# The input projection's 36 column chunks: a 512- and a 256-column product per weight tile in place of three of 256 columns, with the two bank halves added on evacuation

## The chip, the cores and the metric

The kernel runs on one core of a Trainium2 chip. The time is device microseconds of that core for one launch; the times below are of three runs, and one further execution was taken with the hardware profiler. TensorE (PE in the rows, its weight loads PEld) multiplies, VectorE (DVE) and ScalarE (ACT) do the elementwise work, SyncE (SP) issues the DMAs, GpSimd (POOL) does almost nothing.

## The reference, cut to what matters

One layer of a hybrid trunk, 256 tokens of width 2048, in float32:

```python
h = _rmsnorm(x, norm_mix[i])
proj = h @ w_in[i]
(s_x, s_z, s_b, s_c, s_dt, g_q, g_k, g_v, g_g, g_gk) = jnp.split(proj, split_pts, axis=-1)
y_ssd = _ssd_mixer(s_x, s_z, s_b, s_c, s_dt, ...)   # causal conv, silu, chunked scan, gate, norm
y_gla = _gla_mixer(g_q, g_k, g_v, g_g, g_gk, ...)   # gated linear attention, 4 heads, norm, gate
x = x + jnp.concatenate([y_ssd, y_gla], axis=-1) @ w_out[i]
h = _rmsnorm(x, norm_ffn[i])
u = _causal_dwconv(h @ ffn_w_up[i], ffn_conv_w[i], ffn_conv_b[i])
gate, val = jnp.split(u, [D_FF], axis=-1)
x = x + (jax.nn.silu(gate) * val) @ ffn_w_down[i]
pg = jax.nn.sigmoid(_rmsnorm(x, norm_ple[i]) @ ple_w_gate[i])
x = x + pg * (p[i] @ ple_w_proj[i])
return _rmsnorm(x, norm_final)
```

## The kernel before, in words

Every projection multiplies float32 numbers as sums of two rounded parts, a high and a low one: hi x hi + hi x lo + lo x hi. Weights arrive in chunks of 1 MB ([128, 2048], sixteen tiles of 128x128 side by side; the "v" chunks are [128, 1408]). `load` fetches a chunk into one of four `raw` buffers and `prepare` splits it in two halves, each with a cast on ACT (L185, `whi`) and a subtraction on DVE (L186, `wlo`); there are five buffers each of `whi` and `wlo`, so five halves. Activations lie as [128, 2, 256] tiles: the high parts of the 256 tokens, and behind them the low parts.

The input projection walks through the list `PLAN`: 12 value chunks "v" (in which the weights are the moving operand, L893 to L895, 352 columns, 24 products in a chunk) and 36 others: conv8 to conv11, conv0, v4, conv1, v5, conv2, v6, conv3, v7, conv4, q0, k0, conv5, v8, conv6, v9, conv7, v10, q1, k1, v11, q2, k2, q3, k3, z0 to z7, g0 to g7. Each of these 36 makes 128 output columns for all tokens, in 16 steps (k0 to k15, one weight tile each) of `mm3`: three products of 256 columns into the first half of a PSUM bank. `mm2`, used in the output, up, down and gate projections that follow, does the same with a 512-column product (hi x both parts, into both halves of the bank) and a 256-column one (lo x hi, into the first half); there `combine` adds the halves, with a copy on ACT (L229) and an add on DVE (L230). When a chunk is done its evacuation runs: `ev_conv` (scale by the norm, causal convolution, L526 to L531, then `half_silu`: tanh L436 on ACT, L437 on DVE), `ev_qk` (L727), `ev_z` (L699), `ev_g` (L838).

Between the steps stand "helper" matmuls of the two mixers and the norms. TensorE's order is fixed by the program: every fourth step calls `tick`, which resumes at most one of the tasks that are due; a task issues its next piece and yields a number of ticks. `mark` makes a result available to waiting tasks some ticks later. So the helper's place in TensorE's row is counted in steps, and TensorE waits there if the operand is late. ACT and DVE are ordered by a scheduler, in which weights (`load`) and norms have priority, and each takes its instructions strictly in that order.

The helpers that the prediction speaks of: the norms (`norm_task`, `gla_token` and `gla_norm`): L285 sums squares over partitions, DVE finds the inverse root with small operations (L288 to L298, then its high and low part L303 and L305), ACT makes two diagonal matrices per part (L310), and two matmuls L318 spread the result over the partitions; behind the norms of the GLA heads DVE scales the head (L807) and `ev_g` multiplies the gate in (L843, then `split`, L265). The decays of the scan (`decay_src`: eight ACT operations L582; `decay`: matmuls L589 and L590, then the exponential L592 on ACT); `decay` number i is followed by the sources of number i + 2. And L600, four transposes of convolved tiles (`ssd_xdt`).

Of the kernel before, what the change touches and what calls it, by code (L numbers as in the profile page):

```python
# [12 lines left out]
ALU = mybir.AluOpType  # L13
PSUM = bass.MemoryType.PSUM

T = 256
KT = 16
# [80 lines left out]
def trunk(ctx, tc, wst, wv, xin, pin, prm_d, cst_d, gku_d, out):  # L98
    nc = tc.nc
    V, S, G, PE = nc.vector, nc.scalar, nc.gpsimd, nc.tensor  # L100
# [15 lines left out]
    def tmp():  # L116
        return small.tile([128, T], F32, name="tmp", bufs=10)
# [31 lines left out]
    def mark(key, lag=5):  # L149
        done[key] = now[0] + lag  # L150
# [59 lines left out]
    def lhs(wt, j):  # L210
        hi, lo = wt[j // 8]
        w = slice((j % 8) * 128, (j % 8 + 1) * 128)
        return hi[:, w], lo[:, w]

    def mm2(ps, wt, j, act, first, last):
        hi, lo = lhs(wt, j)
        both = act.rearrange("p a t -> p (a t)")
        PE.matmul(ps, lhsT=hi, rhs=both, start=first, stop=False)  # L218
        PE.matmul(ps[:, 0:T], lhsT=lo, rhs=act[:, 0, :], start=False, stop=last)  # L219

    def mm3(ps, wt, j, act, first, last):
        hi, lo = lhs(wt, j)
        PE.matmul(ps, lhsT=hi, rhs=act[:, 0, :], start=first, stop=False)  # L223
        PE.matmul(ps, lhsT=hi, rhs=act[:, 1, :], start=False, stop=False)  # L224
        PE.matmul(ps, lhsT=lo, rhs=act[:, 0, :], start=False, stop=last)  # L225

    def combine(ps):
        t = tmp()
        S.copy(out=t, in_=ps[:, T:2 * T])  # L229
        V.tensor_tensor(out=t, in0=ps[:, 0:T], in1=t, op=ALU.add)  # L230
        return t
# [20 lines left out]
    def pcol(i):  # L252
        return prm[:, i:i + 1]
# [114 lines left out]
    for m in range(KT):  # L368
        wt = ready[m // 8]
        if m % 2 == 0:  # L370
            ps = pmt() if m % 4 == 0 else pxt()
# [4 lines left out]
    xa = []  # L376
# [28 lines left out]
    state = {}  # L405
# [116 lines left out]
    cT = slot()  # L522

    def ev_conv(i, ps):
        v = tmp()
        V.tensor_tensor(out=v, in0=ps[:, 0:T], in1=state["rh"], op=ALU.mult)  # L526
        c = tmp()
        S.activation(out=c, in_=v, func=AF.Identity, scale=pcol(P_CW + 36 + i),
                     bias=cbh[:, i:i + 1])
        for s in (1, 2, 3):  # L530
            V.scalar_tensor_tensor(out=c[:, s:], in0=v[:, :T - s],  # L531
                                   scalar=pcol(P_CW + 12 * (3 - s) + i), in1=c[:, s:],
                                   op0=ALU.mult, op1=ALU.add)
        if i < 8:
            if i % 2 == 0:
                state["xs"] = slot()
            ssd_x[i] = state["xs"][:, (i % 2) * T:(i % 2 + 1) * T]
            half_silu(c, ssd_x[i])
        elif i < 10:
            half_silu(c, bT[:, (i - 8) * T:(i - 7) * T])  # L540
        else:
            half_silu(c, cT[:, (i - 10) * T:(i - 9) * T])
        mark(("conv", i), 12)
# [109 lines left out]
    def ssd_front():  # L653
        yield from gates()
        yield from wait(*[("conv", 8 + i) for i in range(4)])
        ssd_bc()
        yield 1
        ssd_bt()
        for g in range(2):
            order = [(hg, c) for hg in (2 * g, 2 * g + 1) for c in range(2)]  # L660
            if g == 1:
                yield from wait(("y", 0))
            decay_src(*order[0])
            decay_src(*order[1])
            yield 3
            for i, o in enumerate(order):
                yield 4
                decay(*o)
                if i < 2:
                    decay_src(*order[i + 2])  # L670
            mark(("mt", g))
# [23 lines left out]

    def ev_z(i, ps):
        assert ("y", i // 4) in done
        zz = tmp()
        V.tensor_tensor(out=zz, in0=ps[:, 0:T], in1=state["rh"], op=ALU.mult)  # L699
        sz = tmp()  # L700
        half_silu(zz, sz)
        V.tensor_tensor(out=ssd_y[i], in0=ssd_y[i], in1=sz, op=ALU.mult)
        if i % 4 == 0:
            ssd_sq[i // 4] = SumSq()
        ssd_sq[i // 4].add(ssd_y[i])
        mark(("z", i), 7)

    def ssd_norm():
        for g in range(2):
# [14 lines left out]

    def ev_qk(dst, i, ps, sc):
        t = dst[i // 2][:, (i % 2) * T:(i % 2 + 1) * T]
        V.scalar_tensor_tensor(out=t, in0=ps[:, 0:T], scalar=sc, in1=state["rb"],  # L727
                               op0=ALU.mult, op1=ALU.mult)

    def gla_scale(h):  # L730
# [103 lines left out]
                yield 2  # L834

    def ev_g(i, ps):
        gg = tmp()
        V.tensor_tensor(out=gg, in0=ps[:, 0:T], in1=state["rh"], op=ALU.mult)  # L838
        sg = tmp()
        half_silu(gg, sg)  # L840
        assert ("o", i // 2) in done
        o = gla["o", i // 2][:, (i % 2) * T:(i % 2 + 1) * T]
        V.tensor_tensor(out=o, in0=o, in1=sg, op=ALU.mult)  # L843
        mix[8 + i] = split(o)
# [16 lines left out]
    for ci, (kind, i) in enumerate(PLAN):  # L861
        if ci == 0:
            late_loads()
        if ci > 2:
            wt = chunk(N_PROJ + ci)
        else:
            wt = ready.pop(N_PROJ + ci)
        if ci == 3:
            late_work()
        if ci >= 6:  # L870
            for o, t in stores[0:2]:
                dma(o, t)
            del stores[0:2]
            ordered[0] = bool(stores)
        if ci == 4:
            start(norm_task(sq_mix, 2048, in_norm, 7))
            start(ssd_front())
            start(ssd_rest())
            start(gla_front())
            start(gla_back())  # L880
            start(ssd_norm())
        if kind == "v":
            nb, kc = divmod(i, 4)
            if kc == 0:
                vps = [pmt(), pmt()]
            for kk in range(4):
                k = kc * 4 + kk
                hi, lo = wt[kk // 2]
                w = slice((kk % 2) * VB, (kk % 2 + 1) * VB)
                for c in range(2):  # L890
                    tk = slice(c * 128, (c + 1) * 128)
                    o = vps[c][:, 0:VB]
                    PE.matmul(o, lhsT=xa[k][:, 0, tk], rhs=hi[:, w], start=k == 0, stop=False)  # L893
                    PE.matmul(o, lhsT=xa[k][:, 0, tk], rhs=lo[:, w], start=False, stop=False)  # L894
                    PE.matmul(o, lhsT=xa[k][:, 1, tk], rhs=hi[:, w], start=False, stop=k == KT - 1)  # L895
                tick()
            if kc == 3:
                pend.append(lambda a=(nb, vps): ev_v(*a))
                flush()
        else:  # L900
            ps = pmt()
            for k in range(KT):
                mm3(ps[:, 0:T], wt, k, xa[k], k == 0, k == KT - 1)
                if k % TICK == TICK - 1:
                    tick()
            pend.append(lambda a=(kind, i, ps): ev_in(*a))
            flush()
# [156 lines left out]
    with tc.high_priority(offset=PRIO):  # L1064
        v, t = [small.tile([128, 2], F32, name=n, bufs=2) for n in ("rv", "rt")]
# [105 lines left out]
```

## Time and profile before

| what | value |
|---|---|
| time, median of 3 runs | 1241.51 us (1240.69 to 1241.93) |
| the profiled execution's own time | 1241.76 us |
| its span | 1240.0 us |
| mean granted clock of TensorE | 0.998 of full |
| busy: PE, PEld, DVE, ACT | 1228.7, 1103.7, 896.3, 692.1 us |
| chain that ended last | 96% PE |

Busy time is the union of an engine's instructions; matmuls overlap, so their durations add up to more, and what counts is the distance from one start to the next. The input projection's matmuls lie between 18 and 314 us of the span, the output projection from 314 to 404, the up and down projections to 1147, the gate to the end.

### The profile page before, as it was taken

The page shows a single profiled execution, that of the slowest core. Times are in us where ns is not written, and L with a number is a line of the kernel's source. Part 1 is how long each engine was busy: PE and PEld are TensorE (multiplying, and loading weights), DVE is VectorE, ACT ScalarE, POOL GpSimd, SP SyncE. Part 2 cuts the span into 40 slices and gives each one's busy share as a digit, 9 for nine tenths or more (in the row PEclk, how much of TensorE's full clock was granted, in tenths as well). Part 3 has the DMA queues.
Part 4 walks back from the last instruction along what each step waited for, and adds up shares of the span by engine and source line. Part 5 has one row for each costly group of instructions (what it writes and reads, how often), then busy time and mean ns, then how long its engine had stood idle before and what let it go on. Part 6 is the DMA issues. An engine that isn't in the chain of part 4 may idle for free.

```text
span 1240.0 us, 19470 instructions
## 1 busy us (share of the span) xinstructions
PE 1228.7 (99%) x7707; PEld 1103.7 (89%) x7707; DVE 896.3 (72%) x1531; ACT 692.1 (56%) x1144; POOL 3.0 (0%) x10
## 2 busy tenths in 40 slices
PE   9999999999999999999999999999999999999997
PEld 7999999999888888888888888888888888888886
DVE  7877565778677788887786555788777886666775
ACT  8685564566455565555553333555555554444664
POOL 0000000000000000000000000000000000000000
PEclk9999999999999999999999999999999999999999
DMA  8745353445555555555555555555555555556531
GB/s 328 297 144 194 129 203 108 160 147 176 194 176 198 174 200 182 192 197 180 201 179 195 191 183 203 176 198 188 186 200 177 201 183 208 196 179 228 198 134 68
DMA packets 36829, 231.00 MB, mean 186 GB/s; under 512 B 4209, under 2 KB 4593, under 8 KB 11138
## 3 DMA queue, kind: packets, MB, share of 16 engines
q1 hardware_dynamic: 36738, 229.76, 52.3%
q8 instruction: 60, 0.98, 0.3%
q14 instruction: 31, 0.25, 0.1%
HBM read 225.55 MB, written 4.19 MB: 185 GB/s over the span
## 4 chain that ended last, share of the span: by engine, by line
PE 96%; ACT 1%; DVE 1%; DMA 1%; SPq 0%; issue 0%; DVEq 0%
PE pm_t L218 49%; PE pm_t L219 24%; PE pm_t L223 6%; PE pm_t L225 6%; PE pm_t L224 6%; PE pm_t L894 1%; PE pm_t L895 1%; PE pm_t L893 1%; DMA raw<-in_wst_dram 1%; PE px_t L626 1%; ACT xg L257 0%; ACT whi L185 0%; PE px_t L789 0%; ACT tmp L278 0%; PE px_t L285 0%; SPq L165 0%
## 5 line engine op out<-in xcount | busy, mean ns | idle before, releaser
L185 ACT CAST whi<-raw 128x1024 fp32r<-128x1024 f32 (+3 forms) x444 | 443.4, 1004 | 498.5 <-PE pm_t L218 391.3
L186 DVE TENSOR_TENSOR wlo<-raw,whi 128x1024 fp32r<-128x1024 f32 (+3 forms) x444 | 517.3, 1168 | 259.2 <-ACT whi L185 253.7
L218 PE MATMUL pm_t<-xg,whi 128*128 128x512 f32 x1648 | 572.0, 394 | 0.0
L219 PE MATMUL pm_t<-xg,wlo 128*128 128x256 f32 x1648 | 456.6, 277 | 0.0
L218 PEld LDWEIGHTS pm_t<-xg,whi 128*128 128x128 f32 x1648 | 309.0, 188 | 71.6
L218 PE MATMUL pm_t<-slot,whi 128*128 128x512 f32 x960 | 334.6, 395 | 0.0
L219 PEld LDWEIGHTS pm_t<-xg,wlo 128*128 128x128 f32 x1648 | 309.4, 188 | 0.0
L219 PE MATMUL pm_t<-slot,wlo 128*128 128x256 f32 x960 | 266.9, 278 | 0.0
L218 PEld LDWEIGHTS pm_t<-slot,whi 128*128 128x128 f32 x960 | 180.1, 188 | 42.5
L219 PEld LDWEIGHTS pm_t<-slot,wlo 128*128 128x128 f32 x960 | 180.5, 188 | 0.0
L223 PE MATMUL pm_t<-xg,whi 128*128 128x256 f32 x592 | 170.1, 287 | 0.0
L225 PE MATMUL pm_t<-xg,wlo 128*128 128x256 f32 x592 | 167.4, 283 | 0.0
L224 PE MATMUL pm_t<-xg,whi 128*128 128x256 f32 x592 | 167.4, 283 | 0.0
L223 PEld LDWEIGHTS pm_t<-xg,whi 128*128 128x128 f32 x592 | 113.0, 191 | 1.2 <-issue 1.0
L224 PEld LDWEIGHTS pm_t<-xg,whi 128*128 128x128 f32 x592 | 113.0, 191 | 0.4 <-issue 0.2
L225 PEld LDWEIGHTS pm_t<-xg,wlo 128*128 128x128 f32 x592 | 113.0, 191 | 0.0
L959 DVE SCALAR_TENSOR_TENSOR tmp<-tmp,prm 128x255 f32<-128x255 f32 (+1 forms) x176 | 84.7, 481 | 4.5 <-ACT tmp L956 1.5
L914 DVE TENSOR_TENSOR x<-x,pm_t 128x256 f32<-128x256 f32 x96 | 40.1, 419 | 24.3 <-PE pm_t L219 23.0
L956 ACT ACTIVATE tmp<-tmp,prm 128x256 f32<-128x256 f32 x88 | 52.7, 598 | 1.1 <-DVE tmp L954 1.0
L230 DVE TENSOR_TENSOR tmp<-pm_t,tmp 128x256 f32<-128x256 f32 x103 | 43.0, 418 | 0.7 <-ACT tmp L229 0.7
L229 ACT COPY tmp<-pm_t 128x256 f32<-128x256 f32 x103 | 37.4, 364 | 1.3 <-PE pm_t L219 1.3
L954 DVE TENSOR_TENSOR tmp<-tmp,rb 128x256 f32<-128x256 f32 x88 | 37.1, 421 | 1.4
(206 smaller groups left out, 753.3 us busy)
## 6 DMA issues: line engine op xcount, KB each, us to landing
raw<-in_wst_dram SPq DMA_DIRECT2D x200, 1024.0 KB, 4.9
raw<-in_wv_dram SPq DMA_DIRECT2D x8, 704.0 KB, 4.0
raw<-in_wv_dram SPq DMA_DIRECT2D x8, 352.0 KB, 8.3
x<-in_xin_dram SPq DMA_DIRECT2D x4, 512.0 KB, 8.3
pp<-slot SPq DMA_DIRECT2D x8, 256.0 KB, 9.3
slot<-pp SPq DMA_DIRECT2D x8, 256.0 KB, 4.5
out_dram<-raw SPq DMA_DIRECT2D x8, 256.0 KB, 3.2
raw<-in_wst_dram SPq DMA_DIRECT2D x2, 512.0 KB, 8.0
```

What stands on the lines that cost most here:

```text
L185: S.copy(out=hi[:, sl], in_=raw[:, rs])
L186: V.tensor_tensor(out=lo[:, sl], in0=raw[:, rs], in1=hi[:, sl].bitcast(F32), op=ALU.subtract)
L218: PE.matmul(ps, lhsT=hi, rhs=both, start=first, stop=False)
L219: PE.matmul(ps[:, 0:T], lhsT=lo, rhs=act[:, 0, :], start=False, stop=last)
L223: PE.matmul(ps, lhsT=hi, rhs=act[:, 0, :], start=first, stop=False)
L224: PE.matmul(ps, lhsT=hi, rhs=act[:, 1, :], start=False, stop=False)
L225: PE.matmul(ps, lhsT=lo, rhs=act[:, 0, :], start=False, stop=last)
L229: S.copy(out=t, in_=ps[:, T:2 * T])
L230: V.tensor_tensor(out=t, in0=ps[:, 0:T], in1=t, op=ALU.add)
L914: V.tensor_tensor(out=x[:, i, :], in0=x[:, i, :], in1=ps[:, h * T:(h + 1) * T], op=ALU.add)
L956: S.activation(out=c, in_=v, func=AF.Identity, scale=pcol(P_FW + 176 + ch), bias=pcol(P_FB + ch))
L959: V.scalar_tensor_tensor(out=c[:, s:], in0=v[:, :T - s], scalar=pcol(P_FW + 88 * (2 - s) + ch), in1=c[:, s:], op0=ALU.mult, op1=ALU.add)
```

## The change

The 36 chunks use `mm2` in place of `mm3`, four evacuations begin with `combine`, and two lags are longer: the decays begin three ticks later, and the norm of the SSD half starts three ticks later behind its z chunks.

```diff
 def ev_conv(i, ps):
-        v = tmp()
-        V.tensor_tensor(out=v, in0=ps[:, 0:T], in1=state["rh"], op=ALU.mult)
+        v = combine(ps)
+        V.tensor_tensor(out=v, in0=v, in1=state["rh"], op=ALU.mult)
...
             decay_src(*order[1])
-            yield 3
+            yield 6
...
 def ev_z(i, ps):
-        zz = tmp()
-        V.tensor_tensor(out=zz, in0=ps[:, 0:T], in1=state["rh"], op=ALU.mult)
+        zz = combine(ps)
+        V.tensor_tensor(out=zz, in0=zz, in1=state["rh"], op=ALU.mult)
...
-        mark(("z", i), 7)
+        mark(("z", i), 10)
...
 def ev_qk(dst, i, ps, sc):
-        V.scalar_tensor_tensor(out=t, in0=ps[:, 0:T], scalar=sc, in1=state["rb"],
+        V.scalar_tensor_tensor(out=t, in0=combine(ps), scalar=sc, in1=state["rb"],
...
 def ev_g(i, ps):
-        gg = tmp()
-        V.tensor_tensor(out=gg, in0=ps[:, 0:T], in1=state["rh"], op=ALU.mult)
+        gg = combine(ps)
+        V.tensor_tensor(out=gg, in0=gg, in1=state["rh"], op=ALU.mult)
...
             for k in range(KT):
-                mm3(ps[:, 0:T], wt, k, xa[k], k == 0, k == KT - 1)
+                mm2(ps, wt, k, xa[k], k == 0, k == KT - 1)
```

TensorE's rows fall from 7504 to 6928; ACT's rise from 913 to 952 and DVE's from 1388 to 1432 (a row can stand for several alike). In TensorE's order the first decays (L589, L590) move from the starts of v6, conv3, v7 and conv4 to behind the 12th k-step of the same chunks (in a value chunk: its 18th product), the second group from v10, q1, k1 and v11 (k12 each) to the k8 of q1, k1, v11 and q2. L318 of the later norms stood at z5 k8, z6 k0, g0 k0, g3 k8, g4 k0 and g4 k4, and stands at z5 k0, z5 k8, g0 k12, g3 k0, g3 k8 and g4 k12.

ACT's order around the sources of the third decay, which TensorE now needs in v7. Before, the first decay's exponential L592 and the eight L582 of the third decay's sources (`a_hi` and `a_lo` are the two parts of the decay rates) stand between two casts for value chunks:

```order
L185 CAST whi<-raw 128x1024 x2
L185 CAST whi<-raw 128x704
L592 ACTIVATE slot<-px_t 128x512
L582 ACTIVATE slot<-cst,a_hi 128x128 x4
L582 ACTIVATE slot<-cst,a_lo 128x128 x4
L528 ACTIVATE tmp<-tmp,cbh,prm 128x256
```

Now:

```order
L185 CAST whi<-raw 128x1024
L436 ACTIVATE tmp<-tmp 128x256
L229 COPY tmp<-pm_t 128x256
L592 ACTIVATE slot<-px_t 128x512
L582 ACTIVATE slot<-cst,a_hi 128x128 x4
L582 ACTIVATE slot<-cst,a_lo 128x128 x4
```

The same L592 and L582 stand behind a cast of q0's first half, a tanh, and the new copy of conv3's bank.

ACT's order around the decay at k1 and the tanh of conv7, whose result L600 transposes at v11's start. Before:

```order
L592 ACTIVATE slot<-px_t 128x512
L582 ACTIVATE slot<-cst,a_hi 128x128 x4
L582 ACTIVATE slot<-cst,a_lo 128x128 x4
L185 CAST whi<-raw 128x704 x2
L436 ACTIVATE tmp<-tmp 128x256
L592 ACTIVATE slot<-px_t 128x512
```

Now:

```order
L185 CAST whi<-raw 128x1024 x2
L592 ACTIVATE slot<-px_t 128x512
L582 ACTIVATE slot<-cst,a_hi 128x128 x4
L582 ACTIVATE slot<-cst,a_lo 128x128 x4
L436 ACTIVATE tmp<-tmp 128x256
L229 COPY tmp<-pm_t 128x256
```

The L436 of conv7 stood ahead of the L592 of this decay, and stands behind it and its eight L582.

DVE's order in the g chunks, around the scaling of the GLA heads 2 and 3 (L807 twice per head). Before, the parts L303 and L305 of the last norm are made ahead of head 2's L807:

```order
L303 CAST rh_3549<-rr 128x2
L186 TENSOR_TENSOR wlo<-raw,whi 128x1024
L305 TENSOR_TENSOR rl_3551<-rr,rh_3549 128x2
L437 SCALAR_TENSOR_TENSOR tmp<-tmp 128x256
L807 TENSOR_TENSOR slot<-slot,px_t 128x256 x2
L843 TENSOR_TENSOR slot<-slot,tmp 128x256
```

Now head 2's L807 comes first, with the low half of a weight chunk (L186) and the new add L230 behind it:

```order
L807 TENSOR_TENSOR slot<-slot,px_t 128x256 x2
L843 TENSOR_TENSOR slot<-slot,tmp 128x256
L297 TENSOR_TENSOR rt<-rt,rv 128x2
L298 SCALAR_TENSOR_TENSOR rr<-rt,rr 128x2
L186 TENSOR_TENSOR wlo<-raw,whi 128x1024
L230 TENSOR_TENSOR tmp<-pm_t,tmp 128x256
```

Then two more small steps and L265, and behind these:

```order
L838 TENSOR_TENSOR tmp<-tmp,rh 128x256
L303 CAST rh_3065<-rr 128x2
L297 TENSOR_TENSOR rt<-rt,rv 128x2
L186 TENSOR_TENSOR wlo<-raw,whi 128x1024
L305 TENSOR_TENSOR rl_3067<-rr,rh_3065 128x2
```

So L303 and L305 of head 3's norm moved from ahead of the L807 pair to behind it and two L186.

## Rows read from the trace of the kernel before

**Rows 1.** The page: busy us of each engine with its share of the span and its instructions, and the shares of the chain that ended last.

```profile
PE 1228.7 (99%) x7707; PEld 1103.7 (89%) x7707; DVE 896.3 (72%) x1531; ACT 692.1 (56%) x1144; POOL 3.0 (0%) x10
...
PE 96%; ACT 1%; DVE 1%; DMA 1%; SPq 0%; issue 0%; DVEq 0%
```

**Rows 2.** What TensorE waited for, whole span: us in total, how often, the longest.

```profile
PE pm_t L894 <- DVE wlo L186: 0.7, 2, 0.4
```

**Rows 3.** Timeline of TensorE, first step of the last sixty in the old form, and the matmul that follows the last of them (the output projection's first). Columns: start us, duration us, engine, line, operation, out<-in.

```profile
292.26 0.28 PE L223 MATMUL pm_t<-xg,whi 128*128 128x256 f32 x1
...
313.86 0.40 PE L218 MATMUL pm_t<-slot,whi 128*128 128x512 f32 x1
```

**Rows 4.** Timeline of TensorE in the output projection, two 512-column products sixty steps apart.

```profile
340.00 0.40 PE L218 MATMUL pm_t<-slot,whi 128*128 128x512 f32 x1
...
361.20 0.40 PE L218 MATMUL pm_t<-slot,whi 128*128 128x512 f32 x1
```

**Rows 5.** Timeline of TensorE in the up projection, around a norm's L285.

```profile
414.08 0.28 PE L219 MATMUL pm_t<-xg,wlo 128*128 128x256 f32 x1
414.20 0.50 PE L285 MATMUL px_t<-cst,acc 128*128 128x1 f32 x4
414.56 0.48 PE L218 MATMUL pm_t<-xg,whi 128*128 128x512 f32 x1
```

**Rows 6.** Timeline of TensorE in the up projection, two 512-column products sixty steps apart.

```profile
599.66 0.39 PE L218 MATMUL pm_t<-xg,whi 128*128 128x512 f32 x1
...
620.46 0.39 PE L218 MATMUL pm_t<-xg,whi 128*128 128x512 f32 x1
```

**Rows 7.** The page's costliest groups: line, engine, operation, shapes, count, then busy us and mean ns of one, then idle time before them and what ended it.

```profile
L230 DVE TENSOR_TENSOR tmp<-pm_t,tmp 128x256 f32<-128x256 f32 x103 | 43.0, 418 | 0.7 <-ACT tmp L229 0.7
L229 ACT COPY tmp<-pm_t 128x256 f32<-128x256 f32 x103 | 37.4, 364 | 1.3 <-PE pm_t L219 1.3
```

**Rows 8.** Groups by line and form, 36 to 260 us, same columns.

```profile
L436 ACT ACTIVATE tmp<-tmp 128x256 f32<-128x256 f32 x19 | 7.9, 414 | 3.7 <-DVE tmp L531 3.6
...
L437 DVE SCALAR_TENSOR_TENSOR slot<-tmp 128x256 f32<-128x256 f32 x12 | 5.1, 422 | 1.3 <-ACT tmp L436 1.3
```

**Rows 9.** Timelines of TensorE's weight loads, ACT and DVE around L318 of the first norm, at conv10's start; in brackets the idle time before an instruction and what ended it.

```profile
48.32 0.19 PEld L318 LDWEIGHTS px_t<-diag,ones_r 128*128 128x128 f32 x1 [0.17 <-ACT diag L310]
...
42.95 1.05 ACT L185 CAST whi<-raw 128x1024 fp32r<-128x1024 f32 x1 [2.39 <-DMA raw<-in_wst_dram]
45.28 1.05 ACT L185 CAST whi<-raw 128x1024 fp32r<-128x1024 f32 x1 [1.27 <-DVE wlo L186]
46.23 0.69 ACT L310 ACTIVATE diag<-cst,rh 128x128 fp32r<-128x128 f32 x2
46.82 0.27 ACT L455 ACTIVATE dtg<-pm_t,rtk 128x32 f32<-128x32 f32 x1
...
45.18 0.15 DVE L298 SCALAR_TENSOR_TENSOR rr<-rt,rr 128x2 f32<-128x2 f32 x1
```

**Rows 10.** Timelines of TensorE and ACT at the first decay of the scan, at v6's start.

```profile
89.05 0.39 PE L590 MATMUL px_t<-slot,usuf_r 128*128 128x512 f32 x1
89.28 0.32 PE L893 MATMUL pm_t<-whi,xg 128*128 128x352 f32 x1
89.44 0.32 PE L894 MATMUL pm_t<-wlo,xg 128*128 128x352 f32 x1
...
89.58 0.59 ACT L592 ACTIVATE slot<-px_t 128x512 f32<-128x512 f32 x1
90.07 1.27 ACT L582 ACTIVATE slot<-cst,a_hi 128x128 fp32r<-128x128 f32 x4
...
92.41 0.59 ACT L528 ACTIVATE tmp<-tmp,cbh,prm 128x256 f32<-128x256 f32 x1
```

**Rows 11.** Timelines of TensorE and DVE in the g chunks, around L318 of head 2's norm.

```profile
287.25 0.40 PE L318 MATMUL px_t<-diag,ones_r 128*128 128x256 f32 x2
...
279.77 1.23 DVE L186 TENSOR_TENSOR wlo<-raw,whi 128x1024 fp32r<-128x1024 f32 x1
280.91 0.15 DVE L295 SCALAR_TENSOR_TENSOR rt<-rr 128x2 f32<-128x2 f32 x1
...
286.72 0.15 DVE L305 TENSOR_TENSOR rl<-rr,rh 128x2 fp32r<-128x2 f32 x1
...
287.68 0.75 DVE L807 TENSOR_TENSOR slot<-slot,px_t 128x256 f32<-128x256 f32 x2 [0.48 <-PE px_t L318]
288.35 0.42 DVE L843 TENSOR_TENSOR slot<-slot,tmp 128x256 f32<-128x256 f32 x1
288.69 1.22 DVE L186 TENSOR_TENSOR wlo<-raw,whi 128x1024 fp32r<-128x1024 f32 x1
```

**Rows 12.** Busy us of each engine (and its instructions) in the stretch from 270 to 300 us, after the stretch's length; then the granted clock, the DMA share and GB/s.

```profile
270.00:300.00 30.00, 30.00 (x253) 30.00 (x253) 27.87 (x86) 19.08 (x40) 0.00 (x0) 1.00 0.49 172
```

**Rows 13.** Timeline of TensorE at the start of the program.

```profile
1.26 1.04 PE L346 MATMUL px_t<-slot 128*128 128x512 bf16 x2 [1.26 <-DVE slot L343]
...
5.51 0.41 PE L225 MATMUL pm_t<-slot,wlo 128*128 128x256 f32 x1
...
5.93 0.41 PE L224 MATMUL pm_t<-slot,whi 128*128 128x256 f32 x1
...
6.55 0.28 PE L224 MATMUL pm_t<-slot,whi 128*128 128x256 f32 x1
```

## The prediction

> **What bounds the kernel now.** I read the busy times first: TensorE is busy 1228.7 of 1240.0 us and the chain that ended last runs through it for 96% [rows 1]. The list of what it waited for comes next: past the start of the program its largest entry is 0.7 us, in two waits of at most 0.4 [rows 2]. So a nanosecond per matmul counts in full, and so does every wait that the change puts ahead of one. The reader is to look for two things, then: the start-to-start time of matmuls in the old and in the new form, and whether each helper matmul (norm, decay, transpose) still finds its operands ready.
>
> **The gain in the 36 chunks.** Each weight tile ("step") now takes three 256-column products. Sixty steps run from 292.26 to 313.86, 360.0 ns each [rows 3]. The new form, a 512- and a 256-column product, already runs in the later projections, and there in two rhythms. From 340.00 to 361.20 sixty steps take 21.20 us, 353.3 ns each [rows 4]; from 599.66 to 620.46 sixty take 20.80 us, 346.7 ns each [rows 6]. I call them A and B. A begins where the output projection follows the last chunk with no matmul between [rows 3] and holds until the L285 products at 414.20; the next step starts at 414.56 and B holds from there [rows 5]. I take it from this that B is what follows a break by helper matmuls, and A what is entered without one. In the changed program's order 472 of the 576 steps follow a helper, and 104 follow a value chunk directly. For those I take A, the only entry without a break that the trace shows; B would be the other bound. So 472 x 13.3 ns + 104 x 6.7 ns = 6.28 + 0.70 = 6.97 us. All in B would be 7.66, all in A 3.86.
>
> The Trainium skill, "TensorE: Matmul & The Clock Gate", section "Back-to-back issue gap", speaks against so much: it gives an isolated gap of N/2.4 + 2.5 ns, so by it the old step is 327.5 ns, the new 325.0, and the 36 chunks save an estimated 1.4 us. The measured 360.0 against 346.7 and 353.3 disagrees with it in the size of the saving [rows 3, 4, 6].
>
> **The gain in the output projection.** Before, the 284 steps from 313.86 to 414.20 (its 256, and the up projection's first 28) go in A. Now the last GLA norm's L318 stands in g4's k12, so that chunks g5 to g7 and the output projection come after a break. If B is kept from there, 284 x 6.7 ns = 1.89 us; if not, 0. I take 1.89, since every L285 or L318 break among new-form steps in the trace is followed by B [rows 5].
>
> **What the evacuation adds.** 36 copies on ACT at 364 ns and 36 adds on DVE at 418 ns [rows 7], 13.1 and 15.0 us in all. They lie beside matmuls where these engines have room. The fullest stretch is 270 to 300: DVE busy 27.87 of 30, ACT 19.08 [rows 12]. There five chunks bring 5 x 0.34 = 1.7 us more DVE work. The weight halves are prepared up to five ahead, so I set the throughput at nothing; without that cover it costs the eight g chunks 8 x 0.34 = 2.7 us (a rival below). Order costs more: a helper matmul that stands at a fixed step waits if its operand has been pushed back in ACT's or DVE's queue, and all matmuls behind it wait with it. In the changed order four helpers come late. No transfer is added, and none stands elsewhere in its queue.
>
> *The mix norm, L318 at conv10.* Before, its second weight load already waits 0.17 us for ACT's L310 [rows 9]. What sets this is the landing of a weight chunk that ACT's cast of 42.95 waited 2.39 us for, and DVE's small norm steps around 45.18 behind it. TensorE arrives two chunks of saving earlier, 32 x 13.3 ns = 0.43 us, and finds nothing earlier. The new add of conv8 stands among the norm's steps on DVE, 0.34 us (the spacing of 256-wide work, 288.35 to 288.69 [rows 11]). Together 0.75 us; 0.1 if the DMA lands earlier and the add fits a gap, 1.0 with a copy ahead of it.
>
> *The third decay, L589 and L590 at v7's 18th product.* Its sources are the eight L582. Before, they follow the first decay's exponential (L592) at once, from 90.07 to 92.41 [rows 10], most of three chunks ahead of their use. Now the first decay stands 12 k-steps later, and ACT has ahead of the eight: a cast into a buffer that conv3 frees only at its end, L436, L229 of conv3, and L592. From conv3's end that is 0.95 (45.28 to 46.23 [rows 9]) + 0.32 + 0.27 (L436 and L229, 414 and 364 ns less the 0.09 by which starts run closer, as L592's 592 ns does to 0.49 [rows 7, 8, 10]) + 0.49 + 2.34 + about 0.14 for signals = 4.51 us. TensorE needs L590 after 18 value products at 0.16 and one 512-column product of 0.23, both in [rows 10], = 3.12. Wait: 1.4 us; 1.2 without the signals, 1.8 if the cast starts late.
>
> *L600 at v11's start.* It needs conv7's tanh (L436) and L437, and ACT now has L592 and eight L582 of the decay at k1's k8 ahead of L436. From that L590's start: 0.44 (90 ns of signal less, its own 0.39 [rows 10] as a bound) + 0.49 + 2.34 + 0.41 + 0.42 [rows 8, 10] = 4.10. TensorE gets there in 0.23 + 8 x 0.347 + two transposes of 0.12 = 3.25. Wait: 0.85 us, with 0.7 to 1.0 as bounds.
>
> *L318 at g3's k8, head 3's norm.* Before, DVE has its L303 and L305 behind it before L807 begins [rows 11]. Now they stand behind the two L807 of head 2, which wait for L318 at g3's k0. From that L318's start: 0.43 to L807, 0.67 for the pair, 0.34 L843 [all rows 11], then small steps 0.15, a low half L186 1.14 (279.77 to 280.91 [rows 11]), the add L230 0.34, small steps 0.15, L265 and L838 0.34 each, small steps 0.2, another L186 1.14, L305 0.1; then ACT's two L310, 0.59 (46.23 to 46.82 [rows 9]), and 0.1 for signals: 6.0 us. TensorE needs it after 0.23 + 8 x 0.347 = 3.0. Wait: 3.0 us, the largest. If the second L186 has its place taken by idle time it is 1.9; if it also waits for a cast, 0.95 more, 4.0.
>
> Waits: 0.75 + 1.4 + 0.85 + 3.0 = 6.0 us, from 4.0 to 7.8 with the bounds. Two more helpers have little to spare in the new order (L559 at v5's start, and the last half of the mixed tiles in the output projection); I set both at nothing, at most 1 us.
>
> **Sum.** The profiled execution took 1241.76 us, 1240.0 of span and 1.76 around it, 0.25 above the median of the runs. 1241.76 - 6.97 - 1.89 + 6.0 = 1238.9; on the median's footing 1238.65, so **1238.7 us**. Its own range, with waits of 4.0 to 8.8 and the first gain up to 7.66: 1236.0 to 1241.5.
>
> **The rivals.**
> - *The waits are not there.* The lags were lengthened, and each wait is a difference of two sums of some 3 to 6 us; if ACT or DVE are idle earlier than I think, the norm's steps are done in time. All gone: 1241.5 - 8.9 = 1232.6; half of them: 1235.7. Against it: the order at g3 leaves no freedom, since DVE takes its rows in turn.
> - *Rhythm A everywhere* (ends on the other side). If what makes B is not the break but something of the later projections, all 576 steps save 6.7 ns and the output projection nothing: 8.86 - 3.86 = 5.0 us less gain, 1243.7. It decides when more than 425 of the 756 steps (472 + 284) stay in A, since 425 x 6.7 ns is the 2.8 us of my forecast. For it: the first 284 new-form steps of the trace are all A [rows 4]; against it, the break at 414.20 [rows 5].
> - *The clock falls in the wait at g3.* The kernel's start shows what a fall costs: two 256-column products take 0.42 us at 5.51, the lower level of 1.2 GHz, and 0.12 each at the higher [rows 3, 13]; that lasts from 1.26 to about 6.5, and 5.2 us x (1 - 0.12/0.21) = 2.2 us. With no wait over 0.4 us past the start [rows 2], the trace does not show whether 3 us suffices. Time: 1240.9. The Trainium skill, same page, section "Why this matters for your kernels", says that idle gaps between bursts can bring TensorE back to the lower clock; no row here tests that.
> - *DVE becomes the bound in the g chunks*: 2.7 us as worked out above, 1241.4. For it the 27.87 of 30 [rows 12]; against it, the output projection's start is not held back by what g leaves over.
> - *Only a fixed cost per matmul is saved*: 576 x 2.5 ns = 1.4 us and nothing in the output projection, with the waits 1246.1. The 13.3 ns between the rows of [rows 3] and [rows 6] deny it.
>
> **How the numbers follow.** Forecast as summed 0.53 (over half of it below 1239.0); waits absent or halved 0.17; A everywhere 0.13; clock 0.07; DVE 0.07; fixed cost 0.03. Within 0.2% of 1241.5 means 1239.0 to 1244.0, about what a measurement of this kernel can tell from no change. Faster: 0.29 + 0.17 = 0.46. Slower: 0.08 of A (some of the unsized helpers late too) + 0.03 = 0.11. Same: 0.43. The range reaches down into the halved waits and up to A: 1234.8 to 1243.5.
>
> **What would show it.** Right: steps of 346.7 ns in most of conv to g and in the output projection; TensorE waits of about 0.7, 1.4, 0.85 and 3.0 us at conv10, v7, v11 and g3, each put down to ACT's L582, L436/L437 or L310. The granted clock stays at the higher level (2.4 GHz). Wrong: steps of 353.3 ns after helper breaks; no wait over 1 us; a wait of TensorE for L185 or L186 in the g chunks, which would be the DVE rival; products 0.2 us apart after g3, the clock. The forecast falls most easily at g3, where one wait is half of all losses.

## The result, and the profile after

The changed kernel took **1256.44 us in the median of 20 runs, from 1242.33 to 1262.09**, against 1241.36 us (1240.69 to 1242.67) for 20 runs of the kernel before. The forecast was 1238.7 us, range 1234.8 to 1243.5. The runs fall into two groups: nine from 1242.33 to 1244.05 us, eleven from 1256.38 to 1262.09. The kernel before has one group. The ratio of the mean times is 1.0067, interval 1.0048 to 1.0087, without the three slowest runs; as a mean over two groups it describes neither. The median of the lower group (1243.26 us) is 0.2% above the kernel before, that of the upper one (1257.60 us) 1.3%. Why one program has two such groups turned out to be the question of this case.

The profiled execution belongs to the upper group: 1258.71 us, span 1256.9, granted clock 0.996. Its page, busy times and the chain that ended last, beside [rows 1]:

```profile
PE 1238.8 (99%) x7131; PEld 1081.4 (86%) x7131; DVE 906.9 (72%) x1567; ACT 701.7 (56%) x1180; POOL 2.8 (0%) x10
...
PE 95%; ACT 2%; DVE 1%; DMA 1%; issue 1%; SPq 0%; DVEq 0%; ACTq 0%
```

TensorE is still the bound, with 576 matmuls fewer and 10 us more busy time: its matmuls stand further apart. What it waited for, beside [rows 2] (us in total, times, longest):

```profile
PE px_t L318 <- ACT diag L310: 2.7, 2, 2.0
...
PE px_t L600 <- DVE slot L437: 1.1, 1, 1.1
...
PE px_t L589 <- ACT slot L582: 0.7, 1, 0.7
PE px_t L590 <- ACT slot L582: 0.7, 1, 0.7
```

These are the late operands that the prediction named: L318 at g3, L600 at v11, and L589 and L590 at v7. But the list explains 5 us, and does not bring the 17 by which the two spans differ. Four instants do, all starts of matmuls: the output projection's first step, the norm's L285 in the up projection, L285 in the gate projection, and the end. The rows of TensorE's timeline after (columns as in [rows 3]):

```profile
315.94 0.39 PE L218 MATMUL pm_t<-slot,whi 128*128 128x512 f32 x1
...
414.40 0.50 PE L285 MATMUL px_t<-cst,acc 128*128 128x1 f32 x4
...
1161.32 0.50 PE L285 MATMUL px_t<-cst,acc 128*128 128x1 f32 x4
```

and the last of the three in the kernel before (the first two are in [rows 3, 5]):

```profile
1147.04 0.50 PE L285 MATMUL px_t<-cst,acc 128*128 128x1 f32 x4
```

| stretch | before, us | after, us | difference |
|---|---|---|---|
| start to the output projection | 313.86 | 315.94 | +2.08 |
| to L285 in the up projection (284 steps) | 100.34 | 98.46 | -1.88 |
| to L285 in the gate projection (2112 steps) | 732.84 | 746.92 | +14.08 |
| to the end | 92.96 | 95.58 | +2.62 |
| span | 1240.0 | 1256.9 | +16.9 |

The products that the change rewrites all lie in the first line. The third, 14.08 us, lies in the up and down projections, where TensorE's instructions are the same. Two products sixty steps apart there, beside [rows 6]:

```profile
600.21 0.40 PE L218 MATMUL pm_t<-xg,whi 128*128 128x512 f32 x1
...
621.41 0.40 PE L218 MATMUL pm_t<-xg,whi 128*128 128x512 f32 x1
```

They are 21.20 us apart where before they were 20.80: 353.3 ns a step in place of 346.7, rhythm A in place of rhythm B. The 2112 steps times 6.67 ns are 14.08 us, the whole of the line. The gate projection's 212 steps at A add 1.41 to the last line. The other 1.2 us lie behind the last matmul, and 0.7 of them are one place in DVE's order. Before, the last norm's L1072 comes ahead of a copy, L1061:

```profile
1230.74 0.16 DVE L1072 TENSOR_TENSOR rt<-rt,rv 128x2 f32<-128x2 f32 x1
...
1231.01 0.68 DVE L1061 COPY slot<-px_t 128x512 f32<-128x512 f32 x1
```

After, it waits behind the copy, and the scaling of the output with it:

```profile
1246.53 0.69 DVE L1061 COPY slot<-px_t 128x512 f32<-128x512 f32 x1
1247.14 0.15 DVE L1072 TENSOR_TENSOR rt<-rt,rv 128x2 f32<-128x2 f32 x1
```

The remaining 0.5 us, from the scaling to the end, is not followed.

### The profile page after: what moved, and what is told of

Its sections match the earlier page's. It is cut to its first block, busy times and chain, and to the rows that moved or that the text cites. A ratio compares the mean times of both kernels' runs of the same rounds, so it can differ in the third digit from the quotient of the medians.

```text
span 1256.9 us, 18393 instructions
## 1 busy us (share of the span) xinstructions
PE 1238.8 (99%) x7131; PEld 1081.4 (86%) x7131; DVE 906.9 (72%) x1567; ACT 701.7 (56%) x1180; POOL 2.8 (0%) x10
## 4 chain that ended last, share of the span: by engine, by line
PE 95%; ACT 2%; DVE 1%; DMA 1%; issue 1%; SPq 0%; DVEq 0%; ACTq 0%
PE pm_t L218 59%; PE pm_t L219 30%; PE pm_t L894 1%; PE pm_t L895 1%; PE pm_t L893 1%; DMA raw<-in_wst_dram 1%; PE px_t L626 1%; ACT whi L185 1%; ACT xg L257 0%; ACT slot L582 0%; PE px_t L789 0%; ACT tmp L278 0%; DVE wlo L186 0%; PE px_t L285 0%; SPq L165 0%
## 5 line engine op out<-in xcount | busy, mean ns | idle before, releaser
L218 PE MATMUL pm_t<-xg,whi 128*128 128x512 f32 x2224 | 790.6, 400 | 0.0
L186 DVE TENSOR_TENSOR wlo<-raw,whi 128x1024 fp32r<-128x1024 f32 (+3 forms) x444 | 516.9, 1167 | 281.6 <-ACT whi L185 274.8
L218 PEld LDWEIGHTS pm_t<-xg,whi 128*128 128x128 f32 x2224 | 418.9, 188 | 101.3 <-issue 1.2
L230 DVE TENSOR_TENSOR tmp<-pm_t,tmp 128x256 f32<-128x256 f32 x139 | 58.0, 417 | 0.7 <-ACT tmp L229 0.7
L229 ACT COPY tmp<-pm_t 128x256 f32<-128x256 f32 x139 | 50.2, 361 | 1.3 <-PE pm_t L219 1.3
L893 PE MATMUL pm_t<-whi,xg 128*128 128x352 f32 x96 | 32.3, 336 | 0.3 <-ACT whi L185 0.3
L894 PE MATMUL pm_t<-wlo,xg 128*128 128x352 f32 x96 | 31.3, 326 | 0.8 <-DVE wlo L186 0.6
L279 DVE TENSOR_TENSOR acc<-acc,tmp 128x256 f32<-128x256 f32 x69 | 28.8, 418 | 3.9 <-ACT tmp L278 3.9
L895 PE MATMUL pm_t<-whi,xg 128*128 128x352 f32 x96 | 31.0, 322 | 0.0
L278 ACT ACTIVATE tmp<-x 128x256 f32<-128x256 f32 x59 | 23.1, 407 | 4.8 <-DVE x L1007 4.8
L257 ACT ACTIVATE xg<-x,prm 128x256 fp32r<-128x256 f32 x48 | 23.1, 507 | 0.0
```

What stands on the lines that cost most here:

```text
L186: V.tensor_tensor(out=lo[:, sl], in0=raw[:, rs], in1=hi[:, sl].bitcast(F32), op=ALU.subtract)
```

## The experiments

To tell rhythms apart I read the starts of successive 512-column products from the trace in nanoseconds. There are three forms of these distances. Rhythm A repeats every three: 350, 350, 361. Rhythm B comes **even** (346, 347, 347) or **alternating** (343, 350). A "break" is a place where helper matmuls stand between two steps. "Just ahead" of a break means the last distance between two such products ahead of it, "one back" and "two back" the distances before that one. The last product, which has the break behind it, has no distance of its own.

### Are the waits the ones that were named, and what do they cost?

One edit takes away the wait at g3 alone, by moving the norms of GLA heads 2 and 3 later:

```diff
                 gla_token(h)
                 yield 4
-            yield 4
+            yield 4 if b == 0 else 7
```

> The changed kernel with three ticks more ahead of the norms of GLA heads 2 and 3, so that L318 stands later and finds its operand. Expected of the waits: those at v7 (1.8 us) and v11 (1.3) stay, that at g3 (3.2) goes. Theory 'a wait of 3 us drops the clock': the stretch of 0.64 us per step behind it goes too, the granted clock is 0.998 in every run, another 2.2 us less. Theory 'inherited': without the fall of the clock the rhythm of the long stretch is the same in all runs, one group: 1256.5 - 3.2 = 1253.3 us if it is the 353.3 ns rhythm, 1238.0 if it is 346.7. Rival 'chance at the break': two groups, 1238 and 1253.

Measured: 1253.55 us (1253.16 to 1254.16), clock 0.998 in each run, one group; L318 is gone from the list of waits and the other three stand there as before. The expected 1253.3 came out.

Another takes all three away, by one tick more between the decays:

```diff
             for i, o in enumerate(order):
-                yield 4
+                yield 5
                 decay(*o)
```

> The changed kernel with five ticks in place of four between the decays of the scan, which moves the helpers behind them. Expected: none of the waits at v7, v11 and g3 is left (6.2 us by the trace of the changed kernel), no fall of the clock, granted clock 0.998. Theory 'inherited': one group, at 1256.5 - 6.2 = 1250.3 us with the long stretch at 353.3 ns or at 1235.0 with 346.7. Rival 'chance at the break': both groups. If the waits only move elsewhere, the time stays within 1 us of the changed kernel's groups (1243, 1257).

Measured: 1249.85 us (1249.74 to 1251.56), one group, with none of the three waits left. Against the six of the 20 runs of the change that have a clock of 0.998 (1256.38 to 1257.60 us, median 1256.66) that is 6.8 us less: about 6.2 for the three waits, and 0.7 behind the last matmul, since in this run's trace L1072 stands ahead of the copy again. So the waits cost about what was forecast, and were not the surprise: without any of them the kernel is still 8.4 us slower than before, at rhythm A from L285 on.

### What decides the rhythm of 2300 steps that the change does not touch?

Theory: it is handed on from what runs ahead. First test: enter the output projection from three products of 256 columns, as before.

```diff
             for k in range(KT):
-                mm2(ps, wt, k, xa[k], k == 0, k == KT - 1)
+                if (kind, i) == ("g", 7):
+                    mm3(ps[:, 0:T], wt, k, xa[k], k == 0, k == KT - 1)
+                else:
+                    mm2(ps, wt, k, xa[k], k == 0, k == KT - 1)
```

> The changed kernel with its last input chunk, g7, in three products of 256 columns again (and without the add of halves for it), so that the output projection is entered from the old form as in the kernel before. All waits of the changed kernel stay (v7, v11, g3). Theory 'inherited': the rhythm of the up and down projections (2300 steps) follows from the state in which the output projection is entered, through the same L285 break; the old form gives one fixed state. Then the output projection runs at 353.3 ns, the up and down projections at 346.7 ns in every run, one group of times at about 1258.7 - 15.3 + 1.9 + 0.1 = 1245.4 us (1244 to 1248 with the scatter of the clock's fall). Rival 'chance at the break': the L285 break itself picks the rhythm, so the times still fall into two groups, near 1245 and near 1260.

Measured: 1260.61 us (1259.32 to 1262.09), one group, the upper one. The forecast of 1245.4 was wrong, and so was the rival's two groups. The same with five ticks between the decays:

> Both edits together: five ticks between the decays, and g7 in three products of 256 columns. Theory 'inherited': no waits, no fall of the clock, the output projection at 353.3 ns, the up and down projections at 346.7 ns in every run: 1235.0 + 1.9 + 0.2 = 1237.1 us, one group, below both kernels. Rival 'chance at the break': two groups, 1237 and 1252.

Measured: 1252.53 us (1252.09 to 1253.04): one group, and again with the long stretch at A: the forecast of 1237.1 was wrong too. The output projection ran at A in both, as before the change, and the rhythm of the output projection alone therefore does not decide.

The difference lies in where the break comes in A's pattern of three. In the kernel before, the distance just ahead of L285 is one of 361 ns. Here the pattern starts one step off (351, 361, 349 behind the old form, where it was 352, 341, 351, 361), and the 361 ns distance is two back. I therefore counted, over the breaks in the traces at hand, what form stands ahead and what follows. This is the count over all 17 traces of the study, breaks at which TensorE did not wait, with at least five new-form steps ahead and four behind:

| ahead of the break | behind L285 (4 products) | behind L318 (2 products) |
|---|---|---|
| A, 361 ns distance just ahead | B alternating, 8 of 8 | A, 6 of 6 |
| A, 361 ns distance one back | (once, too short to tell) | B alternating, 18 of 18 |
| A, 361 ns distance two back | A, 33 of 33 | A, 34 of 34 |
| B alternating | B alternating, 31 of 31 | B alternating, 24 of 24 with 343 ns just ahead; B even, 17 of 17 with 350 ns just ahead |
| B even | A, 11 of 11 | B even, 6 of 6 |

The outcome follows from the form and the place in its pattern in every row. In the traces of the runs without the wait at g3 (that wait alone removed, or five ticks between the decays) that keep g7 in the new form, it is an L318 in the g chunks with 350 ns just ahead that turns alternating into even, the form that the next L285 turns into A.

The count over the first six traces (14 of 14, 13 of 13, 6 of 6) gave the next four expectations. If the rhythm follows from the place in the pattern, a norm's matmuls moved by four steps must turn it.

```diff
-            yield 6
-            yield from norm_task(sq, 2048, then)
+            yield first
+            yield from norm_task(sq, 2048, then, lag)
...
-    norm_then(sq_ffn)
+    norm_then(sq_ffn, 6, 5)
```

That is the edit of the first (on top of five ticks between the decays); the others use (6, 7), the kernel before with (8, 6), and the changed kernel as it is with (6, 5).

> The kernel with five ticks between the decays, and the FFN norm's lag 5 in place of 6: its L318, in the up projection, stands 20 steps behind L285 in place of 24. Nothing before it moves. Theory 'inherited': a break's outcome follows from the rhythm and the place in its three-step pattern (350, 350, 361 ns) at which it comes. In the six traces so far L318 after a 361 ns step one back gave 346.7 ns (6 of 6), after one two back 353.3 ns (13 of 13). At 24 steps it is two back, at 20 one back. So the stretch behind L318 runs at 346.7 ns in every run: 1249.9 less 2300 x 6.67 ns = 15.3, 1234.5 us, below both kernels. Rival 'chance at the break': two groups, 1234.5 and 1249.9. Rival 'the up projection itself prefers 353.3 ns after this change': 1249.9 in every run.

Measured: **1234.48 us** (1234.20 to 1235.18), one group; ratio to the kernel before 0.9946, interval 0.9933 to 0.9960. The break in its trace:

```profile
412.56 0.40 PE L218 MATMUL pm_t<-xg,whi 128*128 128x512 f32 x1
...
412.92 0.40 PE L218 MATMUL pm_t<-xg,whi 128*128 128x512 f32 x1
...
413.27 0.40 PE L218 MATMUL pm_t<-xg,whi 128*128 128x512 f32 x1
...
413.62 0.39 PE L318 MATMUL px_t<-diag,ones_r 128*128 128x256 f32 x2
...
600.36 0.40 PE L218 MATMUL pm_t<-xg,whi 128*128 128x512 f32 x1
...
621.16 0.40 PE L218 MATMUL pm_t<-xg,whi 128*128 128x512 f32 x1
```

The distances ahead of L318 are 0.36 and 0.35 us, so the long one is one back, and behind it sixty steps take 20.80 us. One number, four steps: 15.4 us between this run and the one without it.

> The same with lag 7, L318 28 steps behind L285, as far on the other side. Theory 'inherited': L318 comes straight behind a 361 ns step, which gave 353.3 ns in 2 of 2 breaks so far: 1249.9 us, one group. If any move of L318 brings the faster rhythm: 1234.5.

Measured: 1248.81 us (1248.37 to 1249.53), one group, rhythm A to the gate. It is 1.1 us less than expected since L285 in the gate came with the 361 ns distance just ahead, so that its last 212 steps ran at B (1.4 us).

> The kernel before, unchanged but for two ticks more ahead of the FFN norm: its L285 stands at 292 steps behind the output projection's start in place of 284. No product changes its form and the input projection is the same. Theory 'inherited': at 284 steps the break comes straight behind a 361 ns step (which gave 346.7 ns), at 292 two steps behind one (353.3 ns in 14 of 14 breaks so far), so the long stretch falls into 353.3 ns in every run: 1241.4 + 2300 x 6.67 ns = 1256.7 us. Rival 'the slow rhythm comes from the changed input projection': 1241.4 us as before.

Measured: 1255.67 us (1255.53 to 1256.13), one group: the kernel before becomes 14.4 us slower though none of its products changes. The gate's 212 steps run at B here too, the 1.4 us that were expected and did not come. The rows around its L285, and sixty steps behind it:

```profile
415.28 0.40 PE L218 MATMUL pm_t<-xg,whi 128*128 128x512 f32 x1
...
415.64 0.40 PE L218 MATMUL pm_t<-xg,whi 128*128 128x512 f32 x1
...
415.99 0.40 PE L218 MATMUL pm_t<-xg,whi 128*128 128x512 f32 x1
...
416.34 0.40 PE L218 MATMUL pm_t<-xg,whi 128*128 128x512 f32 x1
...
416.70 0.50 PE L285 MATMUL px_t<-cst,acc 128*128 128x1 f32 x4
...
600.40 0.40 PE L218 MATMUL pm_t<-xg,whi 128*128 128x512 f32 x1
...
621.60 0.40 PE L218 MATMUL pm_t<-xg,whi 128*128 128x512 f32 x1
```

The distances are 0.36, 0.35, 0.35, the long one two back, and the sixty steps take 21.20 us, as in the changed kernel.

> The changed kernel with the FFN norm's lag 5 alone; the waits at v7, v11 and g3 and the clock's fall stay. Theory 'inherited': whatever rhythm the output projection is left in after the clock's fall (346.7 ns in both of its forms, seen as 346/347 or as 343/350), the long stretch ends at 346.7 ns: one group, the lower one of the changed kernel, 1243.3 us (1242 to 1246). Rival 'chance at the break': both groups, 1243 and 1257 to 1262.

Measured: 1243.57 us (1241.53 to 1246.35, 11 runs), none near the upper group. Moving the FFN norm's L318 by four steps is enough to remove the upper group with everything else as in the change.

### The two groups of one program

Six more executions of the changed kernel were traced.

> The changed kernel once more, for a trace. Theory 'inherited': if the long stretch runs at 353.3 ns (time about 1256 to 1262), the L285 break behind the output projection comes in an even 346/347 ns rhythm or two steps behind a 361 ns step; if at 346.7 (1242 to 1244), in the alternating 343/350 ns form or straight behind a 361 ns step. Rival 'chance at the break': the same rhythm ahead of the break with the other outcome behind it.

> The same as the run before, for another draw: what is ahead of the L285 break decides what is behind it.

> The changed kernel, another execution with a trace. Theory 'inherited': time 1242 to 1244 us with the alternating 343/350 ns form, or the last step of 361 ns, ahead of the L285 break at about 414 us; 1256 to 1262 us with the even 346/347 ns form or a 361 ns step two back. What is ahead differs between the two groups from the first steps behind g3's late L318 on, where the clock comes up again at a moment of its own. Rival 'chance at the break': the same form ahead, the other outcome.

> As e12_draw: another execution of the changed kernel with a trace.

> As e12_draw: another execution of the changed kernel with a trace.

> As e12_draw: another execution of the changed kernel with a trace.

| run | us | clock at 290 to 292 us | form at the end of the output projection | long stretch |
|---|---|---|---|---|
| changed kernel, first trace | 1258.71 | 0.50 | B even | A |
| e10 | 1256.68 | 1.00 | B even | A |
| e11 | 1258.52 | 1.00 | B even | A |
| e12 | 1258.16 | 0.50 | B even | A |
| e13 | 1256.38 | 1.00 | B even | A |
| e14 | 1244.02 | 0.50 | B alternating | B |
| e15 | 1260.76 | 0.52 | A, 361 ns distance two back | A |

Each outcome is the one that the break table gives for what stands ahead, and in all of them L318 at g3 waited about 3 us. Ahead of that wait the seven traces agree (alternating, at g3's first eight steps). Behind it they part. In e10, e11 and e13, where the granted clock stayed at 1.00, the steps came out even. (In e11 part of the wait still lies in this stretch, as it came to g3 1.8 us later than e10: 1.0 at its first conv chunk already, and 0.8 in a longer wait for L318 at conv10.) In the others it fell, in e12 two steps behind L318; the stretch from 290 to 292 us of the first trace (columns as in [rows 12]):

```profile
290.00:292.00 2.00, 2.00 (x8) 1.72 (x7) 0.85 (x4) 1.11 (x4) 0.00 (x0) 0.50 0.99 401
```

and the same stretch of e13:

```profile
290.00:292.00 2.00, 2.00 (x14) 1.75 (x13) 0.00 (x0) 0.98 (x2) 0.00 (x0) 1.00 0.72 303
```

0.50 is the lower level, 1.2 GHz, and 8 matmuls lie in the stretch in place of 14. The steps of e14 and e15 behind g3's L318 are 640 ns for four steps and then, in nanoseconds, 410 and 350 in the one, 422 and 348 in the other; the first goes on alternating, the second at A. In the first trace they are four times 640, then 447 and 352, and even. So where the clock comes up again in the middle of a step differs from run to run, and the form behind it differs with it; that the one causes the other is argued from these few cases and not tested. What sets the moment stays open. Among the first 20 runs, the six with a clock of 0.998 are all in the upper group; of the seven traces, those without a fall show 0.998 and those with one 0.996 or 0.997.

The lower group of the change is thus a by-product of the worst wait: with that wait alone removed, four of four runs kept the long stretch at A (1253.16 to 1254.16 us), and in the traces of the changed kernel the alternating form came out only where the clock fell.

### The lags alone

> The changed kernel with both lags as before (decays begin after 3 ticks, z's mark at 7). By the new order the sources of the fourth decay (L582) are late for conv4's start, about 4.0 + 0.95 us, and the sum for g1's L285 by about 1.3; the waits at v7, v11 and g3 are gone: 6.3 us of waits in place of 6.2. Theory: the lags move waits and do not remove them; the time is 1249.9 + 6.3 = 1256.2 us with the long stretch at 353.3 ns, or 1240.9 at 346.7, and 1 to 3 us more if the clock falls in the 5 us at conv4. Rival 'the longer lags cause the loss': below 1240.

Edit: `yield 6` and `mark(("z", i), 10)` back to 3 and 7. Measured: 1257.79 us (1256.76 to 1260.49), clock 0.996; waits of 3.8 us at L589, 0.7 at L590, and 0.9 at L285 in the list, none at L318. The longer lags only move the waits. One tick in another place (five between the decays) removes them.

## Why the prediction was wrong

**The failing step is "I take it from this that B is what follows a break by helper matmuls".** It made the rhythm a property of the break alone. The runs show that what follows a break depends on the form and on the place in the pattern of three at which it comes, and that the state is carried over hundreds of steps. [rows 5] was one case: A with the 361 ns distance just ahead, which gives B. Even B, the form in which the changed kernel's output projection ran, gives A at the same L285. The trace of before could not show that, since no new-form step ran in even form there. It did show A and B in a kernel whose later projections are alike, and I priced A only for the 756 steps I took to be in play: the 2300 steps behind L285, which the change does not touch, stood in no term. The rival "rhythm A everywhere" looked at the right quantity, but with a third of the size and another mechanism. It put B down to the later projections themselves, and these are what ran at A. With A in the 2300 steps the sum is 1238.7 + 15.4 = 1254.1 us with no other term changed, and none of the range reached there.

**The sum to the output projection** was -0.97 us (-6.97 + 6.0) and measured +2.08. The step that begins conv8 came 0.26 us earlier (35.86 against 36.12 us; over the 17 traces it lies between 34.87 and 36.45), which no term had. The rest is in three terms:

- *The first gain* was 5.3 us, not 6.97. In the trace of the changed kernel it is what is left of +2.08 when the 0.26, the waits and the fall of the clock are taken out. Without waits (five ticks between the decays, lag 5) it shows directly. The first step of conv8 before, and that step and the output projection's first in that run:

```profile
36.12 0.28 PE L223 MATMUL pm_t<-xg,whi 128*128 128x256 f32 x1
```

```profile
35.11 0.39 PE L218 MATMUL pm_t<-xg,whi 128*128 128x512 f32 x1
...
307.66 0.39 PE L218 MATMUL pm_t<-slot,whi 128*128 128x512 f32 x1
```

From the one to the other it is 272.55 us, and was 277.74 with the 313.86 of [rows 3]: 5.2 us. In runs of five or more steps 308 of 516 steps of the changed kernel were at B and 236 of 508 in this run, where I took 472 of 576. By these shares the gains would be 6.1 and 5.6 us; the rest is not followed.

- *The waits* came out at 6.3 us in all, where 6.0 was summed, in part by luck: v7, v11 and g3 took 1.8 (0.84 ahead of L589 and 0.94 ahead of L590), 1.3 and 3.2 us where the sum has 1.4, 0.85 and 3.0, and the one at v11 lies outside its bounds. The rest, at conv10, makes up for it near its lower bound of 0.1: L318 and what follows it took 0.57 us (47.41 to 47.98) where 0.47 stood before; in e11 and e14 it was near the upper one, 0.9. At v7 and g3 the rows say what was worked out. ACT after, at v7:

```profile
98.43 1.05 ACT L185 CAST whi<-raw 128x1024 fp32r<-128x1024 f32 x1 [2.05 <-issue]
99.39 0.41 ACT L436 ACTIVATE tmp<-tmp 128x256 f32<-128x256 f32 x1
99.70 0.35 ACT L229 COPY tmp<-pm_t 128x256 f32<-128x256 f32 x1
99.95 0.60 ACT L592 ACTIVATE slot<-px_t 128x512 f32<-128x512 f32 x1
100.44 1.27 ACT L582 ACTIVATE slot<-cst,a_hi 128x128 fp32r<-128x128 f32 x4
101.61 1.27 ACT L582 ACTIVATE slot<-cst,a_lo 128x128 fp32r<-128x128 f32 x4
```

TensorE there, v7's first product and the late L590:

```profile
98.02 0.32 PE L893 MATMUL pm_t<-whi,xg 128*128 128x352 f32 x1
...
102.93 0.50 PE L590 MATMUL px_t<-slot,usuf_r 128*128 128x512 f32 x1 [0.67 <-ACT slot L582]
```

The cast, the tanh, the copy, the exponential, the eight: the order ahead of the wait, at the spacings of [rows 8 to 10]. From the cast's start to L590 it is 4.50 us, and 4.51 was summed. What is more than 1.4 us of wait is that the cast starts 0.41 us behind v7's first product, the late cast of the upper bound. DVE and TensorE after, at g3:

```profile
283.21 0.75 DVE L807 TENSOR_TENSOR slot<-slot,px_t 128x256 f32<-128x256 f32 x2
...
287.00 1.23 DVE L186 TENSOR_TENSOR wlo<-raw,whi 128x1024 fp32r<-128x1024 f32 x1
288.14 0.15 DVE L305 TENSOR_TENSOR rl<-rr,rh 128x2 fp32r<-128x2 f32 x1
...
287.92 0.38 PE L318 MATMUL px_t<-diag,ones_r 128*128 128x256 f32 x1 [1.98 <-ACT diag L310]
289.08 0.58 PE L318 MATMUL px_t<-diag,ones_r 128*128 128x256 f32 x1 [0.77 <-ACT diag L310]
```

From the L807 pair to L305 it is 4.93 us; with 0.43 ahead and ACT's L310 behind, about the 6.0 of the sum.

- *The fall of the clock* was a rival at 0.07 and came in four of the seven traces. It cost less than the 2.2 us of that rival: four steps at 640 ns and one at 447, 1.3 us over 346.7. The Trainium skill, "TensorE: Matmul & The Clock Gate", section "Why this matters for your kernels", warns of it for idle stretches between bursts; the trace agrees in the direction, with a granted clock of 0.50 behind 3.2 us of waits, and shows that the same waits left it at 1.00 in other runs (e10, e11, e13).

**The gain in the output projection** came out to 0.01 us: 1.88 measured, 1.89 forecast, in the B that I had counted on. With the rule behind it wrong that was luck; in e15 the output projection ran at A. That very B, in its even form, led to the A behind L285 that cost 15.4 us.

**Evacuation at nothing** held: no wait of TensorE for a cast or a low half appears in the z and g chunks. DVE as the bound did not come. The fixed cost per matmul as the only saving did not either: without waits 5.2 us were gained where 1.4 would have been.

**What beats both kernels** is the change with five ticks between the decays and lag 5 for the FFN norm, 1234.48 us. In its trace the span is 7.5 us shorter than before: 6.2 up to the output projection (1.0 of them already there at conv8's first step) and 1.9 in it, less 0.1 for twenty steps at A and 0.5 behind the gate's L285.

## What to carry to other kernels

Where TensorE is the bound and its stream is uniform, measure the start-to-start time in each long stretch and not only where an edit falls: an edit far ahead can change the rhythm of a stretch that it does not touch, here by 2% of 750 us. When one program's times fall into groups, compare the traces of two groups for the first place at which they part, then move a break by a few steps to see whether the outcome follows. A helper matmul's late operand is found by walking the queue order of the engine that makes it, with spacings from the trace, to within some tenths of a microsecond.

## What the runs showed of the hardware

A 512- and a 256-column product in turn have two lasting rhythms, 346.7 and 353.3 ns a pair, at the same granted clock of 1.00. Which of them holds is set anew at breaks by other matmuls and then lasts, for 2088 steps in one piece. At a break without a wait the outcome follows from the form ahead of it and from the place in that form's pattern, in all 188 breaks of the table. Three products of 256 columns showed one rhythm, 360.0 ns. Why there are two rhythms, and why the second has a pattern of three steps, stays open: no run here reaches below the starts of matmuls. A TensorE that waits 3.2 us in two parts may come back at the lower clock level or not: of the seven traces of the changed kernel three show a clock of 1.00 behind the wait and four one of 0.50 to 0.52.
